# Three-piece float32 products on one Trainium2 core: the order of the products that share a weight tile

## The chip, the cores and the metric

The kernel runs on one NeuronCore of a Trainium2 chip. The metric is the device time of one launch in microseconds. The core's engines appear under their profile names: PE (TensorE, matrix products; PEld is its load of the stationary operand), DVE (VectorE), ACT (ScalarE), POOL (GpSimd) and SP (SyncE, which here only issues transfers).

## The reference

One layer of a bidirectional encoder over 256 tokens, all in float32, with model width 2048. Cut to its large products:

```python
h  = rmsnorm(x, mix_norm_pre)               # (256, 2048)
u  = h @ w_in                               # z 1024 | xbc 1536 | dt 32, pooling 1024
y  = cat(ssd_both_directions(u), pooled(u)) # (256, 2048): state space heads and pooling
x  = x + rmsnorm(y @ w_out, ...)
h  = rmsnorm(x, ...)
g, v = split(h @ w_ffn_up)                  # 2 x 5632
f  = gelu(conv3(g)) * v                     # (256, 5632)
x  = x + rmsnorm(f @ w_down, ...)
gate = sigmoid(rmsnorm(x, ...) @ w_ple_gate) # (256, 2048), computed with a tanh
out = x + rmsnorm(gate * (p @ w_ple), ...)
```

The weights come from HBM; the result must agree with the float32 reference closely.

## The kernel before

**Three products for one.** PE multiplies in a rounded float32 format. To keep float32 accuracy, every operand is split into a high part (the value rounded to that format) and a low part (the remainder). `split()` (L142 to L155) does it for a weight tile: ACT copies the raw tile into the high tile (L153), DVE subtracts that from the raw tile and gets the low tile (L154). High and low tiles come from two rings of five buffers each, the raw tiles from a ring of three that transfers on SP's queue fill. A product x·w is then the sum of three in PSUM: xh·wh, xh·wl and xl·wh. The product xl·wl is left out. `mm()` (L89 and L90) issues each of them; the profile therefore shows nearly all matmuls at L90 and tells them apart by their tiles. Names end in h and l: `dn_0h` is the high part of a w_down tile.

**The stages in time.** dtu (0 to 53 us; dt and pooling inputs, a loop of its own), xbc (53 to 143 us, with the small products of the state space part, such as seg, placed between), z (143 to 198 us), w_out (198 to 287 us, tiles woa, wos), ple and the transposes woxt, the up projection ga/va (293 to 788 us, `feature_pairs`), w_down (788 to 1011 us, tiles dna, dns, dn0s, dn1s), ple and the transposes dnxt, w_gate (1017 to 1106 us, tiles gt, gts), and the last norm with the output.

**feature_major** (L339 to L353) makes xbc with features on the partitions: the weight is the stationary operand, and the moving one is 256 tokens wide. A k tile gives 4 feature blocks of three products, 12 matmuls.

**token_major** (L305 to L337) makes z, w_out, ple, w_down and w_gate with 128 tokens on the partitions, in two token tiles t: a piece of x is stationary, and 512 columns of the weight move. Per half of 1024 columns, a k tile is 2 token tiles × 3 products × 2 column blocks, 12 matmuls. The variable q numbers the products: 0 is xh·wh, 1 is xh·wl, 2 is xl·wh. The last unit of a half (and the one that follows the last fast unit) runs instead bank by bank, over all k tiles of its group.

**seven_products** (L255 to L281) is used for the fast units of w_out, w_down and w_gate: seven products of blocks instead of eight, for a pair of k tiles, each in three pieces, 21 matmuls. Weight tiles are a, b, d and c in the order of their splits; b, d and c each serve two of the seven. x comes as the blocks a11, a12, a22 (from the split hidden tile hs, two buffers, written by ACT at L928 and DVE at L929) and the sums s1 to s4 (tile hd). `combine` adds the results up after the last fast unit.

**What sets the order.** The program is written in one order, and a scheduler then orders the instructions of each engine by readiness and priority, so that PE's order in the trace isn't quite that of the loops. Every engine works its list in order.

**The tail.** After w_gate's second half, each bank gets a tanh (ACT, L1154), a product (DVE, L1155), a square with a sum (ACT, L1162, the last one L1160) and a product with the norm's weight (DVE, L1163). `finish(t)` takes the norm of a token tile from POOL (go0m, go0r, L378 to L381; rest_of at L1106 to L1108) and writes vg with four steps on DVE (L1126).

Of the kernel before, what the change touches and what calls it, by code (L numbers as in the profile page):

```python
# [17 lines left out]
P = 128  # L18
L = 256
D = 2048  # L20
NK = D // P
# [32 lines left out]
def build(nc, a, out):  # L54
    x = a["x"][0]
# [5 lines left out]
    with tile.TileContext(nc) as tc, \  # L61
# [9 lines left out]
        def ins(r):  # L71
            return getattr(r, "ins", r)
# [10 lines left out]
        def main(name):  # L83
            return [pm.tile([P, 512], F32, tag="main", name=f"{name}_{i}") for i in range(2)]
# [4 lines left out]
        def mm(o, lhsT, rhs, start, stop):  # L89
            last["pe"] = ins(nc.tensor.matmul(o, lhsT, rhs, start=start, stop=stop, skip_group_check=True))  # L90
# [15 lines left out]
        acc, acc2 = [main(f"dtu{t}") for t in range(2)], main("dtu2")  # L106
# [10 lines left out]
        def load(dst, src, ahead=False):  # L117

            with tc.issue_after(last["dma"]) if last and not ahead else nullcontext():
                return ins(nc.sync.dma_start(dst, src))  # L120
# [36 lines left out]
        def raw(name, src=None):  # L157
            r = wp.tile([P, 2048], F32, tag="raw", bufs=3, name=name)
            if src is not None:
                last["dma"] = load(r, src, True)  # L160
            return r
# [25 lines left out]
        def put(dst, src, scale):  # L187
# [3 lines left out]
                    ins(nc.vector.scalar_tensor_tensor(lo, src, scale, hi.bitcast(F32),  # L191
                                                       op0=ALU.mult, op1=ALU.subtract)))

        work = []

        chain = {}
# [22 lines left out]
        def columns(acc):  # L219

            c = 0
            for o in acc:
                yield o, c
                c += o.shape[-1]
# [30 lines left out]
        def seven_products(name, stage, w, k0, c0, a_, acc, alt, start, stop):  # L255

            if (stage, c0, k0) in sums_:
                r = raw(f"{name}r")  # L260
                last["dma"] = load(r[:, 512:], w[c0 // 1024, k0 // 2][:, 512:], True)
                t, held = sums_[stage, c0, k0]
                if not held:
                    t = page(f"{name}t")
                    last["dma"] = load(t, sums_[stage, c0, k0][0], True)
            else:
                r = t = raw(f"{name}r", w[c0 // 1024, k0 // 2])
            b11 = split(f"{name}a", r[:, 512:1024], 512)
            b2 = split(f"{name}b", r[:, 1024:], 1024)
            if r is t:  # L270
                add_blocks(r)
            t42 = split(f"{name}d", t[:, 1024:], 1024)
            t31 = split(f"{name}c", t[:, :1024], 1024)

            for x, (wh, wl), c, o, own in (
                    ("a11", b11, 0, alt[0], True), ("a12", b2, 0, acc[0][0], False), ("a22", t42, 0, acc[1][0], False),
                    ("s4", b2, 512, acc[0][1], False), ("s2", t42, 512, alt[3], True), ("s1", t31, 512, alt[1], True),
                    ("s3", t31, 0, alt[2], True)):
                xh, xl = a_[x]
                for q, (xx, ww) in enumerate(((xh, wh), (xh, wl), (xl, wh))):  # L280
                    mm(o, xx, ww[:, c:c + 512], own and start and q == 0, own and stop and q == 2)  # L281

        def combine(name, acc, alt, cut):

# [20 lines left out]
        def token_major(name, w, c0, ks, get, acc, tail=1, fast=(), alt=None, sums=None, at=()):  # L305


            group, nu = [], len(ks) // 2
            for u in range(nu):
                if u in at:  # L310
                    at[u]()
                k0 = ks[2 * u]
                if u in fast:
                    if u == fast[0]:
                        alt = alt + [misc(f"{name}s{i}") for i in (2, 3)]
                    seven_products(f"{name}{k0}", name[:2], w, k0, c0, sums(k0), acc, alt, u == fast[0], u == fast[-1])
                    continue
                r = None if f"{name}{k0}_0" in ready else raw(f"{name}r{k0}", w[c0 // 1024, k0 // 2])
                for j in range(2):
                    group.append((k0 + j, *split(f"{name}{k0}_{j}", r and r[:, j * 1024:(j + 1) * 1024], 1024)))  # L320
                if nu - tail <= u < nu - 1:
                    continue

                order = [(t, o, g, q) for t in range(2) for o in columns(acc[t]) for g in group for q in range(3)] \
                    if u == nu - 1 or u - 1 in fast[-1:] else \
                    [(t, o, g, q) for g in group for t in range(2) for q in range(3) for o in columns(acc[t])]
                for t, (o, c), (k, wh, wl), q in order:
                    xh, xl = (v[:, t * P:(t + 1) * P] for v in get(k))
                    xx, ww = ((xh, wh), (xh, wl), (xl, wh))[q]
                    c = (c + 512 * (k + 1)) % 1024  # L330
                    mm(o, xx, ww[:, c:c + o.shape[-1]], k == ks[0] and q == 0, k == ks[-1] and q == 2)
                if u - 1 in fast[-1:]:
                    combine(name, acc, alt, nu - tail == u + 1 and tail > 1)
                group = []
                aside()
            if nu in at:
                at[nu]()  # L337

        def feature_major(name, w, get, acc):  # L339

            for u in range(4):
                r = raw(f"{name}r{u}", w[u])
                for j in range(2):
                    wh, wl = split(f"{name}{u}_{j}", r[:, j * 1024:(j + 1) * 1024], 1024)
                    for kk in range(2):
                        k = 4 * u + 2 * j + kk
                        xh, xl = get(k)
                        for f in range(4):
                            s = slice(kk * 512 + f * P, kk * 512 + (f + 1) * P)
                            for q, (ww, xx) in enumerate(((wh, xh), (wh, xl), (wl, xh))):  # L350
                                mm(acc[f // 2][:, f % 2 * L:(f % 2 + 1) * L], ww[:, s], xx,
                                   k == 0 and q == 0 and f % 2 == 0, k == NK - 1 and q == 2)
                aside()  # L353

        def feature_pairs(n, part, get, acc):
# [98 lines left out]
        for u in range(0, NK, 2):  # L454
            r = [wp.tile([P, 2048], F32, tag="raw", bufs=3, name=f"dtur{u}") if u else r0, page(f"dtur{u + 1}")]
            for j in range(2):
                k = u + j
# [17 lines left out]
            for j in range(2):  # L475
                k = u + j
                with tc.issue_after(front[0]), tc.issue_after(front[1]):
                    wh, wl = split(f"dtu{k}", r[j][:, :1056], 1056, ((352, 704), (704,))[k] if k < 2 else ())
# [480 lines left out]
        parts, slab = [], {}  # L959
# [47 lines left out]
        with in_order():  # L1007
            for _ in range(5):
                next_part()
            for n in range(NPIECES):  # L1010
                s, v, i = blocks[n // 4]
                if n % 4 == 0:
                    acc = main(f"{'gv'[v]}a{s}{i}")
# [117 lines left out]
        for half in range(2):  # L1131

            alt = [] if half else main(f"gts{half}")
            acc = [main(f"gt{half}{t}") for t in range(2)]
            alt += main(f"gts{half}") if half else []
            ks, fast = gt_ks[half], gt_fast[half]
# [7 lines left out]
            for t in range(2):  # L1144
                for n, (o, c0) in enumerate(columns(acc[t])):
                    c1 = c0 + o.shape[-1]
                    c = slice(half * 1024 + c0, half * 1024 + c1)
# [9 lines left out]
                    q = tiny(f"gq{t}{half}{n}", 1)  # L1157
# [84 lines left out]
```

## Time and profile before

| What | Value |
|---|---|
| time, median of 3 runs | 1117.4 us (1116.87 to 1118.18) |
| span of the profiled execution | 1115.6 us |
| granted PE clock, mean | 0.998 |
| PE / PEld busy | 1104.8 / 951.8 us |
| DVE busy | 957.5 us |
| ACT busy | 721.7 us |
| POOL busy | 68.5 us |
| HBM read / written | 297.48 / 48.76 MB |

The page gives the span from the first to the last instruction of one execution, 1115.6 us; that execution's own time isn't listed beside it, and the median of the timed runs is 1.8 us above the span. Busy times are sums over instructions of one engine. A matmul's record is longer than the distance to the next one, because matmuls are pipelined; the distance between starts is what counts. Where the profile shows a wait, it names the engine, tile and line whose end released the waiting instruction.

### The profile page before, as it was taken

How to read it: one execution, taken by the hardware profiler on the slowest of the kernel's cores; microseconds unless marked ns; L12 is line 12 of the kernel's file. 1: busy time of each engine (PE TensorE's matmuls, PEld its weight loads, DVE VectorE, ACT ScalarE, POOL GpSimd, SP SyncE). 2: the span in 40 equal slices, each digit the busy share in tenths (PEclk: the TensorE clock that was granted, in tenths of full speed). 3: DMA queues.
4: the chain of work that ended last, by engine and by line, in shares of the span. 5: the costliest groups of instructions: out<-in, count | busy, mean ns of one | idle time of the engine just before them, and what ended most of it. 6: DMA issues, size and time to landing. Idle time of an engine off the chain costs nothing.

```text
span 1115.6 us, 16022 instructions
## 1 busy us (share of the span) xinstructions
PE 1104.8 (99%) x5948; PEld 951.8 (85%) x5948; DVE 957.5 (86%) x1334; ACT 721.7 (65%) x1048; POOL 68.5 (6%) x140
## 2 busy tenths in 40 slices
PE   9999999999999999999999999999999999999997
PEld 9999988888888888888888888888888888877876
DVE  6478997799868898888888888888899999989895
ACT  6847662555775564665655645657589778867673
POOL 0200000100100000000000000000000000001001
PEclk9999999999999999999999999999999999999999
DMA  9752447454599999999899999999999899996763
GB/s 362 314 194 109 164 156 284 151 189 158 199 362 401 387 378 376 359 375 369 346 377 382 354 380 366 353 391 391 361 379 382 329 343 400 418 376 229 264 237 105
DMA packets 54943, 347.29 MB, mean 311 GB/s; under 512 B 6096, under 2 KB 6992, under 8 KB 20176
## 3 DMA queue, kind: packets, MB, share of 16 engines
q1 hardware_dynamic: 44064, 289.53, 67.3%
q0 software_dynamic: 10368, 56.10, 13.4%
q8 instruction: 47, 0.77, 0.3%
q10 hardware_dynamic: 432, 0.62, 0.2%
q14 instruction: 32, 0.26, 0.1%
HBM read 297.48 MB, written 48.76 MB: 310 GB/s over the span
## 4 chain that ended last, share of the span: by engine, by line
PE 94%; DVE 2%; ACT 1%; DMA 1%; issue 1%; POOL 0%; POOLq 0%; ACTq 0%; DVEq 0%
PE ga L90 22%; PE va L90 22%; PE dna L90 12%; PE woa L90 7%; PE xbc L90 5%; PE gt L90 5%; PE z L90 4%; PE dns L90 4%; PE dtu L90 4%; PE dn0s L90 2%; PE dn1s L90 2%; DMA dtur<-w_dtu 1%; PE pw L90 1%; PE yd L90 1%; PE gts L90 1%
## 5 line engine op out<-in xcount | busy, mean ns | idle before, releaser
L90 PE MATMUL ga<-wox,ug_0h 128*128 128x512 f32 x352 | 125.5, 395 | 0.0
L90 PE MATMUL ga<-wox,ug_1h 128*128 128x512 f32 x352 | 125.1, 394 | 0.0
L90 PE MATMUL va<-wox,uv_1h 128*128 128x512 f32 x352 | 124.8, 393 | 0.0
L90 PE MATMUL va<-wox,uv_0h 128*128 128x512 f32 x352 | 124.8, 393 | 0.0
L90 PE MATMUL ga<-wox,ug_1l 128*128 128x256 f32 x352 | 99.1, 282 | 0.0
L90 PE MATMUL va<-wox,uv_1l 128*128 128x256 f32 x352 | 99.1, 281 | 0.0
L90 PE MATMUL va<-wox,uv_0l 128*128 128x256 f32 x352 | 99.1, 281 | 0.0
L90 PE MATMUL ga<-wox,ug_0l 128*128 128x256 f32 x352 | 99.0, 281 | 0.0
L253 DVE TENSOR_TENSOR dnb<-dnb 128x512 f32<-128x512 f32 x128 | 88.3, 690 | 3.1
L90 PEld LDWEIGHTS va<-wox,uv_1h 128*128 128x128 f32 x352 | 66.1, 188 | 15.0
L90 PEld LDWEIGHTS va<-wox,uv_0h 128*128 128x128 f32 x352 | 66.1, 188 | 15.0
L90 PEld LDWEIGHTS ga<-wox,ug_1h 128*128 128x128 f32 x352 | 66.1, 188 | 15.0
L90 PEld LDWEIGHTS ga<-wox,ug_0h 128*128 128x128 f32 x352 | 66.1, 188 | 14.8
L90 PEld LDWEIGHTS ga<-wox,ug_0l 128*128 128x128 f32 x352 | 66.2, 188 | 0.1
L90 PEld LDWEIGHTS ga<-wox,ug_1l 128*128 128x128 f32 x352 | 66.2, 188 | 0.0
L90 PEld LDWEIGHTS va<-wox,uv_1l 128*128 128x128 f32 x352 | 66.2, 188 | 0.0
L90 PEld LDWEIGHTS va<-wox,uv_0l 128*128 128x128 f32 x352 | 66.2, 188 | 0.0
L928 ACT CAST hs<-hid 128x512 fp32r<-128x512 f32 x44 | 27.3, 621 | 21.9 <-PE dna L90 21.6
L244 POOL DMA_DIRECT2D dns<-dnb x30 | 16.3, 542 | 309.4 <-DVE dnb L253 309.4
L929 DVE TENSOR_TENSOR hs<-hid,hs 128x512 fp32r<-128x512 f32 x44 | 30.1, 685 | 5.9 <-ACT hs L928 5.9
L792 ACT CAST he<-he 128x512 fp32r<-128x512 f32 x13 | 8.1, 621 | 36.6 <-DVE he L791 36.6
L90 PE MATMUL dna<-dn_1h,hs 128*128 128x512 f32 x96 | 30.9, 393 | 0.0
(2242 smaller groups left out, 3214.8 us busy)
## 6 DMA issues: line engine op xcount, KB each, us to landing
dnb<-w_down SPq DMA_DIRECT2D x32, 1024.0 KB, 9.9
dns<-dnb POOLq DMA_DIRECT2D x30, 1024.0 KB, 6.9
hd<-hsum POOLq DMA_DIRECT2D x24, 512.0 KB, 8.3
zr<-w_z SPq DMA_DIRECT2D x8, 1024.0 KB, 4.8
dtur<-w_dtu SPq DMA_DIRECT2D x14, 528.0 KB, 8.9
wo0r<-w_out_ SPq DMA_DIRECT2D x7, 1024.0 KB, 4.8
dn1r<-w_down SPq DMA_DIRECT2D x7, 1024.0 KB, 6.6
hsum<-he POOLq DMA_DIRECT2D x13, 512.0 KB, 7.9
```

The lines of the kernel that those rows point to most:

```text
L90: last["pe"] = ins(nc.tensor.matmul(o, lhsT, rhs, start=start, stop=stop, skip_group_check=True))
L244: nc.gpsimd.dma_start(t, pg[0])
L253: nc.vector.tensor_add(v[:, i], v[:, i], v[:, j])
L792: nc.scalar.copy(o[:, :512], s[:, :512])
L928: nc.scalar.copy(t[:, :512], hid_part(k))
L929: nc.vector.tensor_sub(t[:, 512:], hid_part(k), t[:, :512].bitcast(F32))
```

## The change

Within the instructions that share a weight tile, the products come in another order: xh·wh and xl·wh first for all of them, xh·wl last. `LOW_LAST = (0, 2), (1,)` holds the two groups of q. In token_major a k tile is now, for both token tiles, q = 0 and q = 2 (8 matmuls), then q = 1 (4 matmuls); in bank-by-bank order, each bank takes all k tiles' q = 0 and 2, then all q = 1. feature_major does the same over its 4 feature blocks. In seven_products the list is written out: a11 (0, 2, 1); a12 (0, 2); a22 (0, 2); a12 (1); s4 (0, 2, 1); a22 (1); s2 (0, 2, 1); s1 (0, 2); s3 (0, 2); s1 (1); s3 (1). The flag that ends a PSUM group moves from q = 2 to q = 1. Lines behind the first insertion move down by one to six. dtu, ga/va and everything else keep their order.

```diff
--- before.py
+++ after.py
@@ -191,6 +191,7 @@
                     ins(nc.vector.scalar_tensor_tensor(lo, src, scale, hi.bitcast(F32),
                                                        op0=ALU.mult, op1=ALU.subtract)))
 
+        LOW_LAST = (0, 2), (1,)
         work = []
 
         chain = {}
@@ -272,13 +273,16 @@
             t42 = split(f"{name}d", t[:, 1024:], 1024)
             t31 = split(f"{name}c", t[:, :1024], 1024)
 
-            for x, (wh, wl), c, o, own in (
-                    ("a11", b11, 0, alt[0], True), ("a12", b2, 0, acc[0][0], False), ("a22", t42, 0, acc[1][0], False),
-                    ("s4", b2, 512, acc[0][1], False), ("s2", t42, 512, alt[3], True), ("s1", t31, 512, alt[1], True),
-                    ("s3", t31, 0, alt[2], True)):
+            parts = {"a11": (b11, 0, alt[0], True), "a12": (b2, 0, acc[0][0], False), "a22": (t42, 0, acc[1][0], False),
+                     "s4": (b2, 512, acc[0][1], False), "s2": (t42, 512, alt[3], True), "s1": (t31, 512, alt[1], True),
+                     "s3": (t31, 0, alt[2], True)}
+            for x, qs in (("a11", (0, 2, 1)), ("a12", (0, 2)), ("a22", (0, 2)), ("a12", (1,)), ("s4", (0, 2, 1)),
+                          ("a22", (1,)), ("s2", (0, 2, 1)), ("s1", (0, 2)), ("s3", (0, 2)), ("s1", (1,)), ("s3", (1,))):
+                (wh, wl), c, o, own = parts[x]
                 xh, xl = a_[x]
-                for q, (xx, ww) in enumerate(((xh, wh), (xh, wl), (xl, wh))):
-                    mm(o, xx, ww[:, c:c + 512], own and start and q == 0, own and stop and q == 2)
+                for q in qs:
+                    xx, ww = ((xh, wh), (xh, wl), (xl, wh))[q]
+                    mm(o, xx, ww[:, c:c + 512], own and start and q == 0, own and stop and q == 1)
 
         def combine(name, acc, alt, cut):
 
@@ -321,14 +325,14 @@
                 if nu - tail <= u < nu - 1:
                     continue
 
-                order = [(t, o, g, q) for t in range(2) for o in columns(acc[t]) for g in group for q in range(3)] \
+                order = [(t, o, g, q) for t in range(2) for o in columns(acc[t]) for qs in LOW_LAST for g in group for q in qs] \
                     if u == nu - 1 or u - 1 in fast[-1:] else \
-                    [(t, o, g, q) for g in group for t in range(2) for q in range(3) for o in columns(acc[t])]
+                    [(t, o, g, q) for g in group for qs in LOW_LAST for t in range(2) for q in qs for o in columns(acc[t])]
                 for t, (o, c), (k, wh, wl), q in order:
                     xh, xl = (v[:, t * P:(t + 1) * P] for v in get(k))
                     xx, ww = ((xh, wh), (xh, wl), (xl, wh))[q]
                     c = (c + 512 * (k + 1)) % 1024
-                    mm(o, xx, ww[:, c:c + o.shape[-1]], k == ks[0] and q == 0, k == ks[-1] and q == 2)
+                    mm(o, xx, ww[:, c:c + o.shape[-1]], k == ks[0] and q == 0, k == ks[-1] and q == 1)
                 if u - 1 in fast[-1:]:
                     combine(name, acc, alt, nu - tail == u + 1 and tail > 1)
                 group = []
@@ -345,11 +349,13 @@
                     for kk in range(2):
                         k = 4 * u + 2 * j + kk
                         xh, xl = get(k)
-                        for f in range(4):
-                            s = slice(kk * 512 + f * P, kk * 512 + (f + 1) * P)
-                            for q, (ww, xx) in enumerate(((wh, xh), (wh, xl), (wl, xh))):
-                                mm(acc[f // 2][:, f % 2 * L:(f % 2 + 1) * L], ww[:, s], xx,
-                                   k == 0 and q == 0 and f % 2 == 0, k == NK - 1 and q == 2)
+                        for qs in LOW_LAST:
+                            for f in range(4):
+                                s = slice(kk * 512 + f * P, kk * 512 + (f + 1) * P)
+                                for q in qs:
+                                    ww, xx = ((wh, xh), (wl, xh), (wh, xl))[q]
+                                    mm(acc[f // 2][:, f % 2 * L:(f % 2 + 1) * L], ww[:, s], xx,
+                                       k == 0 and q == 0 and f % 2 == 0, k == NK - 1 and q == 1)
                 aside()
 
         def feature_pairs(n, part, get, acc):
```

## The prediction

> **What bounds the kernel now.** I read the page first (share of each engine, then the chain that ended last), then the waits of TensorE (PE), then the busy time by stretch, and last the rows around each wait of PE.
>
> ```profile
> span 1115.6 us, 16022 instructions
> PE 1104.8 (99%) x5948; PEld 951.8 (85%) x5948; DVE 957.5 (86%) x1334; ACT 721.7 (65%) x1048; POOL 68.5 (6%) x140
> PE 94%; DVE 2%; ACT 1%; DMA 1%; issue 1%; POOL 0%; POOLq 0%; ACTq 0%; DVEq 0%
> ```
>
> PE is busy for 1104.8 of 1115.6 us and carries 94% of the chain. A busy PE can still be a slow one, so its pitch matters. The chain gives unbroken pieces, which I divide by their counts (start, length, engine, tile):
>
> ```profile
> 12.66 40.31 PE dtu L90 x249
> 66.89 5.71 PE xbc L90 x48
> 142.65 22.18 PE z L90 x96
> 886.79 22.15 PE dna L90 x96
> ```
>
> A matmul 512 wide starts every 22.18/96 = 231 ns, one 256 wide every 5.71/48 = 119 ns. The change keeps every matmul with its size, so as long as the pitch holds, only PE's idle time can change: the gaps inside the stages it touches, and the head and tail at either end. These are all the waits of PE (us in total, times, longest):
>
> ```profile
> PE gof L90 <- ACT godg L1117: 1.9, 1, 1.9
> PE dtu L109 <- POOL ident masks.py:199: 1.4, 1, 1.4
> PE gt L90 <- DVE gt_0l L154: 0.8, 1, 0.8
> PE dtu L90 <- DVE dtu2l L154: 0.5, 1, 0.5
> PE gt L90 <- DVE gt18bl L154: 0.4, 1, 0.4
> PE dna L90 <- ACT dn_0h L153: 0.3, 1, 0.3
> PE seg L90 <- ACT E L599: 0.2, 1, 0.2
> ```
>
> The dtu loop at the head isn't touched, and gof is the last product of all. So the change has 0.8 + 0.4 + 0.3 + 0.2 = 1.7 us of visible waiting in its reach. Only two of these waits are for a low part, the thing that it asks for later. The gain is capped near this sum; the loss isn't.
>
> **The change part by part.** No engine gains or loses an instruction: the built kernels hold the same instructions on all five engines, and POOL's and SP's are in the same order, so no DMA is added or moved past another on its queue. What moves is PE's order and, because the scheduler follows PE, parts of DVE's and ACT's.
>
> *Pitch.* The new order changes which operand repeats between neighbours. The pieces above repeat differently: dtu (352 columns) uses each piece of x for three or six matmuls in a row, z for two or four, xbc changes the loaded piece at two of three. Yet they lie on one line: between 119 ns at 256 and 231 ns at 512, it gives 161 ns at 352, and dtu has 40.31/249 = 162 ns, small gaps included. So the order costs nothing that these rows show: 0. The z and dna pieces differ by 0.3 ns a matmul; over the some 2,400 touched ones that would be 0.7 us either way, which I keep for the range.
>
> One rule speaks against the change. In token_major the stationary piece of x now changes six times for each k tile of 12 matmuls instead of four; z has 192/12 = 16 such k tiles. The Trainium skill, TensorE: Matmul & The Clock Gate, "Step-by-step: what each phase is for", says that loads are separate instructions so that one load can serve many matmuls; by it the sum would gain 32 loads in z alone. The rows have no such saving to lose: PEld counts 5948 loads for 5948 matmuls, and they lie beside the matmuls. The sum stays without them.
>
> *Normal k tiles (z, w_out, w_down, w_gate, xbc).* As written, the weight's low part was needed at the third of a k tile's 12 matmuls and is now needed at the ninth: 6 × 231 ns = 1.4 us later in token_major, 6 × 119 ns = 0.7 us in feature_major, less where the scheduler had already moved it. The high tile is free sooner, the low one at most 0.5 us later. Where PE didn't wait, this is worth 0: z, the output projection, most of xbc.
>
> *xbc with seg.* The one wait here is for ACT's E copy, not for a split:
>
> ```profile
> 89.52 0.57 ACT L599 COPY E<-seg 128x512 f32<-128x512 f32 x1
> 90.15 0.50 PE L90 MATMUL seg<-seg_x,seg_w 128*128 128x512 f32 x1 [0.19 <-ACT E L599]
> ```
>
> The built order puts 8 xbc matmuls between the two seg products where 11 stood. PE arrives 3 × 119 ns = 0.36 us sooner at a copy that ACT ends no sooner (it runs back to back there). The wait grows by 0.36 us; bounds 0 and +0.4. I take **+0.36**.
>
> *Seven-product units.* With 21 matmuls (21 × 231 ns = 4.86 us) to a unit, the low parts are asked for as written one to three matmuls later (the scheduler shifts some by one or two). The last use of the hs tile by a22 moves from the 9th to the 12th matmul, 3 × 231 ns = 0.69 us later; ACT's next hs (L928) waits for it.
>
> ```profile
> 788.00:900.00 112.00, 112.00 (x487) 90.97 (x487) 105.46 (x128) 90.66 (x115) 7.02 (x13) 1.00 0.94 356
> 900.00:1000.00 100.00, 99.66 (x431) 80.31 (x430) 93.64 (x115) 78.47 (x97) 6.15 (x11) 1.00 0.99 393
> L928 ACT CAST hs<-hid 128x512 fp32r<-128x512 f32 x44 | 27.3, 621 | 21.9 <-PE dna L90 21.6
> L929 DVE TENSOR_TENSOR hs<-hid,hs 128x512 fp32r<-128x512 f32 x44 | 30.1, 685 | 5.9 <-ACT hs L928 5.9
> ```
>
> The windows give PE, PEld, DVE, ACT and POOL busy, then clock and DMA share. PE fills the down projection while DVE works 94% of it. ACT's wait on PE is long, but the tile is for a later unit, and what DVE loses to it is 5.9 us over 44. In most units the scheduler now puts hs behind the d and c splits instead of ahead of them, so the later release delays nothing: 0. In dn126 to dn132 and dn138 hs still stands ahead; there the splits behind it may come 0.69 us later, but are asked for up to 0.69 us later: 0, with the rival below as the upper bound.
>
> *dn_0h after unit dn132.* This k tile follows a fast unit:
>
> ```profile
> 982.59 0.39 PE L90 MATMUL dn1s<-dn132ch,hd 128*128 128x512 f32 x1
> 983.26 1.20 PE L90 MATMUL dna<-dn_0h,hs 128*128 128x512 f32 x4 [0.28 <-ACT dn_0h L153]
> 984.52 0.73 PE L90 MATMUL dna<-dn_0l,hs 128*128 128x512 f32 x2
> 983.24 1.23 DVE L154 TENSOR_TENSOR dn_0l<-dn1r,dn_0h 128x1024 fp32r<-128x1024 f32 x1 [0.25 <-ACT dn_0h L153]
> ```
>
> From start to start PE loses 0.67 − 0.23 = 0.44 us to the high part. Four matmuls from 983.26 would end near 984.19, but the low part is ready at 984.47: 0.33 us more, of which 0.1 is the restart that both orders have. The low one goes, for eight matmuls now stand ahead of it. The high one shrinks by a matmul, since hs is released one matmul earlier in this unit. Together **−0.55**; bounds −0.77 (all of it) and +0.2 (hi 0.2 later).
>
> *End of w_down, start of w_gate.* Here come ple products, then transposes of the new hb (dnxt), then w_gate:
>
> ```profile
> 1005.27 0.63 PE L90 MATMUL ple<-ple_0h,pth 128*128 128x512 f32 x2
> 1010.59 0.40 PE L90 MATMUL dna<-dn_1h,hs 128*128 128x512 f32 x1
> 1013.86 0.38 PE L391 MATMUL dnxt<-ident,hb 128*128 128x128 f32 x2
> 1021.86 0.72 PE L90 MATMUL gt<-gt_0l,dnxh 128*128 128x512 f32 x2 [0.79 <-DVE gt_0l L154]
> 1020.59 1.22 DVE L154 TENSOR_TENSOR gt_0l<-gt0r,gt_0h 128x1024 fp32r<-128x1024 f32 x1
> ```
>
> Before, 13 ple products stood between w_down's last matmul and the first transpose; now 19 do, 6 × 231 ns = 1.4 us more. w_down's last matmul comes sooner by 0.55 (above), by 0.46 (the two ple products at 1005.27 no longer run inside it) and by an estimated 0.3 (the short stops there for low parts), 1.3 us in all. So the transposes stay within 0.1 us of where they were, and with them DVE's row of hb, dnxl and gt_0l, which ends near 1021.9 instead of 1021.81. PE has two more matmuls behind it when it comes to gt_0l, 0.46 us of work: in all it is 0.4 us ahead after this wait. Of that 0.55 is counted already, so this stage gives **+0.15**, and the saving of w_down's end is spent in a longer wait for gt_0l. Bounds −0.9 (the wait of 0.79 and its restart gone) and +0.9 (transposes 0.8 later).
>
> *gt18.*
>
> ```profile
> 1069.33 0.40 PE L90 MATMUL gts<-gt18ah,dnxl 128*128 128x512 f32 x1
> 1070.17 0.50 PE L90 MATMUL gt<-gt18bl,dnxh 128*128 128x512 f32 x1 [0.45 <-DVE gt18bl L154]
> ```
>
> PE loses 0.84 − 0.23 = 0.61 us and 0.1 at the restart. gt18bl is now asked for after seven matmuls of the unit instead of five, 0.46 us later, so that 0.15 us is left: **−0.55**; bounds −0.7 and −0.3.
>
> *The tail.* The last group of w_gate runs bank by bank. With high parts first and the last raw tile just landing, the built order draws high products of later banks ahead of the low ones of the first. Counting from the end, the banks of token tile 0 finish 1.0 and 2.7 us later than before, the third 0.8 later, the last two at the same place. Their epilogue is a chain of its own, which today runs right up to the end:
>
> ```profile
> 1078.94 16.73 PE gt L90 x73
> 1095.70 0.70 ACT gth L1154
> 1097.15 0.73 ACT gth L1162 x2
> 1098.05 1.07 POOL go0m L378
> 1100.16 2.75 DVE vg L1126 x4
> 1102.90 0.61 DVE gth L1155
> 1106.14 0.55 POOL gth L1108
> 1107.74 0.42 ACT L1160 ACTIVATE gth<-gth 128x257 f32<-128x257 f32 x1 [0.55 <-DVE gth L1155]
> ```
>
> Read from above: banks done, tanh (L1154), square (L1162), POOL's norm, four vg of token tile 0 on DVE, then the last tile's steps. The final square at 1107.74 waits for DVE; POOL's value, which it needs too, is ready at 1106.69, 1.05 us ahead. The first bank is done at 1078.94 + 16.73 = 1095.67 and the second two matmuls later, near 1096.2. With that at 1098.9, its tanh runs at 1099.1, its product and square end near 1101.2, POOL's two last steps near 1102.3: the four vg start 2.1 us late and end at 1105.0. Behind them DVE has the product of the third bank (0.61), one half as wide, and two vg; ACT has two squares ahead of the last tanh, which starts at 1107.0. POOL's value comes at 1108.0, the final square at 1108.0: **+0.28**. Bounds 0 (POOL quicker; the cover is that 1.05 us) and +1.4 (POOL's step as slow as its 1.07 us row once more).
>
> *Sum.* 0.36 − 0.55 + 0.15 − 0.55 + 0.28 = −0.31 us. The span would go from 1115.6 to 1115.3. The median of 1117.4 lies 1.8 us above the profiled span; I take what lies around the span as unchanged. 1117.4 − 0.3 = **1117.1 us**.
>
> **The rivals.** *All waits go.* If the low parts are the whole story and nothing replaces them, the lower bounds add up: −0.77 − 0.9 − 0.7 and 0 elsewhere, and the pitch's −0.7: −3.1 us, 1114.3. For it speaks that two of the four waits are for low parts; against it, that the wait at seg is for a copy, that at dn_0h for a high part, and that the transposes hold gt_0l back. Chance 0.16 for a gain above 0.2%.
>
> *hs starves DVE (slower).* In the fast units of w_down DVE has 0.94 × 4.86 = 4.57 us of work for 4.86 us of PE: 0.29 us to spare. Where hs stands ahead of the splits in ACT's and DVE's queues and its release is 0.69 us later, DVE loses 0.4 us per unit net, and PE waits as soon as the splits' own lead is used up. In the six or so units that keep that order it is some 2.4 us, 1119.8; with restarts and a longer wait at dn_0h about 1120.2; if all 32 fast units behaved so, 13 us, 1130. It decides when DVE's idle time in front of L929 grows from 5.9 us to above 8. Against it: the splits are asked for later by the same 0.69 us, and the scheduler moved hs back in most units. Chance 0.20. Upper bounds falling together at the transposes and in the tail (+0.9 + 1.4 + 0.4) would also pass 0.2%: 0.10.
>
> *It does little.* At dn_0h the scheduler already had four high products ahead of the first low one, half of what the change asks. If it reorders so wherever it matters, the time stays at 1117.4: 0.12.
>
> **How the numbers follow.** Forecast 0.42, no effect 0.12, all waits go 0.16, slower 0.20 + 0.10. A measurement of this kernel tells about 0.2%, 2.2 us, from no change; the forecast and the third rival both lie within it: same 0.54, faster 0.16, slower 0.30. The range: the terms at their upper ends give 0.4 + 0.2 + 0.9 − 0.3 + 1.4 + 0.7 = +3.3 us, 1120.7, which also takes in the six-unit case; at their lower ends the first rival's −3.1, 1114.3. Outside lie the 32-unit case and mixtures, some 0.15.
>
> **What would show it.** In the profile after: the waits for gt18bl and for dn_0l gone or under 0.2 us; the wait for gt_0l still there, at 0.8 to 1.6; seg's wait near 0.5; the four vg at L1132 (the same line, six lower) starting about 2 us later against the last gts product; PE's pitch in z at 231 ns. I am wrong if the pieces of z or dna change their pitch, if DVE's idle time before hs passes 8 us, or if a wait appears in a stage where I put 0.

## The result and the profile after

| What | before | after |
|---|---|---|
| time, median of 14 runs each | 1117.41 us (1116.84 to 1118.52) | 1119.36 us (1118.60 to 1120.46) |
| span of the profiled execution | 1115.6 us | 1117.9 us |
| time of the profiled execution | not listed | 1119.7 us |
| mean span of timed runs | 1115.25 us (108 runs, timed beside the experiments below) | 1117.34 us (the same 14) |

The ratio after to before is 1.0018, with a 95% interval of 1.0011 to 1.0025. The changed kernel is 2 us slower; 1117.1 us, 0.3 us faster, was forecast. The time outside the span scatters by over a microsecond from run to run, so the table of experiments below gives mean spans beside the medians.

The page of the kernel after, its first lines (span, then busy time and count of each engine):

```profile
span 1117.9 us, 16121 instructions
PE 1105.9 (99%) x5948; PEld 951.8 (85%) x5948; DVE 958.0 (86%) x1334; ACT 716.3 (64%) x1048; POOL 68.5 (6%) x140
```

Every engine has the same number of working instructions as before; the 99 that the page counts more are semaphore instructions (DVE has 549 instead of 448, ACT 433 instead of 435). PE has the same 5948 matmuls, yet it is busy 1.1 us longer, and the span grew by 2.3. The busy time alone doesn't show slower matmuls, for the records of matmuls overlap (e9_select below, whose span is shorter than that of the kernel before, has 1105.6 us). The waits and the distances between starts tell more. All waits of PE in the kernel after (us in total, times, longest):

```profile
PE gof L90 <- ACT godg L1123: 2.8, 1, 2.8
PE dtu L109 <- POOL ident masks.py:199: 1.4, 1, 1.4
PE gt L90 <- DVE gt_0l L154: 0.6, 1, 0.6
PE dna L90 <- DVE hs L935: 0.5, 1, 0.5
PE dnxt L397 <- DVE dnxl L191: 0.3, 1, 0.3
PE seg L90 <- ACT E L605: 0.2, 1, 0.2
```

The waits for gt18bl and dn_0h are gone from the list, as forecast (from start to start PE still loses 0.1 and 0.2 us there). A wait for **hs**, the low part of x, is new in the middle of w_down, and the last one, gof, grew from 1.9 to 2.8 us.

PE runs its 5948 matmuls in nearly one order in both kernels, so the start of the matmul at the same position can be compared through the whole span (after minus before; where neighbours are swapped it is good to 0.1 us):

| Stretch (time in the kernel before) | at its end | step |
|---|---|---|
| dtu, to 53 us | −0.52 | −0.52: not reached by the change, see below |
| xbc with seg, to 104 | −0.70 | −0.18 |
| z and w_out, to 273 | −0.73 | −0.03 |
| end of w_out, start of the up projection, to 345 | −0.49 | +0.24 |
| the up projection, to 803 | −0.51 | −0.02 |
| fast units of w_down's first half, 803 to 883 | −0.23 | +0.28 |
| turn from first to second half, 883 to 907 | +0.91 | +1.14 |
| fast units of the second half, 907 to 982.6 | +1.13 | +0.22 |
| dn_0h after dn132 | +0.57 | −0.56 |
| end of w_down, ple, dnxt, gt_0l, to 1032 | +0.83 | +0.26 |
| w_gate to gt18, to 1067 | +0.91 | +0.08 |
| gt18 | +0.44 | −0.47 |
| to the last gts, 1107 | +0.52 | +0.08 |
| tail: to gof | +1.40 | +0.88 |
| last outputs, to the end of the span | +2.29 | +0.9 |

The first step comes mostly from a wait for dtu2l of 0.5 us that the profile of before had and the profile after hasn't, in the dtu loop that neither kernel changes; the other kernels' first stretch differs from before's by +0.04 to −0.85 us, and none of them changes that loop. The last is the final output's transfer, 3.3 us from issue to landing before and 4.2 after; in the other kernels this step lies between −0.4 and +0.2 us. Without these two the change costs 1.9 us, and the mean spans of the runs say 2.1.

**The turn.** PE in the kernel after, around 898 us (start, length, instruction, count, and in brackets the idle time before it and its releaser):

```profile
898.32 0.63 PE L90 MATMUL dna<-dn_0h,hs 128*128 128x512 f32 x2
899.42 1.20 PE L90 MATMUL dna<-dn_0h,hs 128*128 128x512 f32 x4 [0.47 <-DVE hs L935]
```

The same view of the kernel before:

```profile
898.14 0.62 PE L90 MATMUL dna<-dn_0l,hs 128*128 128x512 f32 x2
898.60 0.63 PE L90 MATMUL dna<-dn_0h,hs 128*128 128x512 f32 x2
899.07 0.62 PE L90 MATMUL dna<-dn_0l,hs 128*128 128x512 f32 x2
899.53 1.09 PE L90 MATMUL dna<-dn_0h,hs 128*128 128x512 f32 x4
```

From the two products xh·wh at 898.32 to the next row are 1.10 us for 2 matmuls of 0.23: 0.64 us lost. The four products that wait are xl·wh. Before, four xh·wl (the two rows of dn_0l) stood ahead of them, and they had no wait; now these come behind, so PE asks for xl 4 matmuls, 0.93 us, sooner. With the restart behind it this place costs 0.75 us. Most of the rest of the 1.14 is a stop at 892.5 us, where PE waits 0.2 us for ACT's half of the same kind of split (0.3 us with its restart). DVE of the kernel after in the same stretch:

```profile
896.84 0.75 DVE L845 SCALAR_TENSOR_TENSOR dnm<-dna,rf0r,gffn 128x512 f32<-128x512 f32 x1 [0.29 <-ACT dnj L844]
898.02 0.75 DVE L845 SCALAR_TENSOR_TENSOR dnm<-dna,rf1r,gffn 128x512 f32<-128x512 f32 x1 [0.43 <-ACT dnj L844]
898.69 0.68 DVE L935 TENSOR_TENSOR hs<-hid,hs 128x512 fp32r<-128x512 f32 x1
```

and DVE of the kernel before:

```profile
898.52 0.68 DVE L929 TENSOR_TENSOR hs<-hid,hs 128x512 fp32r<-128x512 f32 x1
```

DVE does not make hs sooner here: the step stands behind the products of the first half's banks with the norm's weight (dnm), and each of those waits for ACT's square of the same bank (dnj). In the kernel before, hs ended at 898.52 + 0.68 = 899.20 and was asked for at 899.53: 0.33 us of slack. The new order asked for 0.93.

### The profile page after: what moved, and what is told of

Read it like the earlier page. It is cut to its first block, busy times and chain, and to the rows that moved or that the text cites. A ratio compares the mean times of both kernels' runs of the same rounds, so it can differ in the third digit from the quotient of the medians.

```text
span 1117.9 us, 16121 instructions
## 1 busy us (share of the span) xinstructions
PE 1105.9 (99%) x5948; PEld 951.8 (85%) x5948; DVE 958.0 (86%) x1334; ACT 716.3 (64%) x1048; POOL 68.5 (6%) x140
## 4 chain that ended last, share of the span: by engine, by line
PE 95%; ACT 1%; DVE 1%; DMA 1%; issue 0%; POOL 0%; POOLq 0%; ACTq 0%
PE ga L90 22%; PE va L90 22%; PE dna L90 12%; PE woa L90 7%; PE gt L90 5%; PE xbc L90 5%; PE z L90 4%; PE dns L90 4%; PE dtu L90 4%; PE dn0s L90 2%; PE dn1s L90 2%; PE ple L90 1%; DMA dtur<-w_dtu 1%; PE pw L90 1%; PE gts L90 1%; PE yd L90 1%
## 5 line engine op out<-in xcount | busy, mean ns | idle before, releaser
L994 ACT ACTIVATE fc<-gr,vt 128x256 f32<-128x256 f32 x44 | 26.1, 593 | 4.1 <-DVE gr L987 4.1
```

The source lines that it names most:

```text
L994: nc.scalar.activation(c[:, f], v[:, f], AF.Identity, bias=vec(V_FCB + 4 * s + 2 * i + f), scale=vec(w + NF))
```

## The experiments

| Run | kernel | median us (before beside it) | ratio, 95% interval | mean span (before 1115.25) |
|---|---|---|---|---|
| e1_seven | new order in seven_products alone | 1118.34 (1117.09) | 1.0013 [1.0004, 1.0021] | 1116.46 |
| e2_token | in token_major alone | 1118.56 (1117.09) | 1.0012 [1.0003, 1.0021] | 1116.35 |
| e3_feature | in feature_major alone | 1116.96 (1117.09) | 0.9998 [0.9989, 1.0007] | 1115.19 |
| e5_dn1_first_old | after, old order at the turn | 1118.84 (1117.17) | 1.0016 [1.0007, 1.0025] | 1116.91 |
| e6_both_old | e5, and the last group of w_gate old | 1119.22 (1117.09) | 1.0018 [1.0009, 1.0026] | 1116.84 |
| e7_both_old_pin | e6, and gof's first pair held at the end | 1118.55 (1117.17) | 1.0013 [1.0004, 1.0021] | 1116.63 |
| e4_tail_old_pin | after, last group old, pair held | 1118.95 (1117.16) | 1.0016 [1.0007, 1.0025] | 1116.99 |
| e8_seven_q021 | before, seven_products in order 0, 2, 1 | 1118.29 (1117.17) | 1.0009 [1.0001, 1.0018] | 1116.27 |
| e10_seven_q102 | before, seven_products in order 1, 0, 2 | 1117.54 (1117.16) | 1.0005 [0.9997, 1.0014] | 1115.91 |
| e9_select | new order at gt18's half and at dn_0h alone | 1116.75 (1117.17) | 0.9995 [0.9986, 1.0004] | 1114.83 |
| e11_select2 | e9, and w_down's last group | 1116.60 (1117.16) | 0.9996 [0.9987, 1.0005] | 1114.89 |
| e12_select3 | e9, and another order in unit dn132 | 1116.10 (1117.15) | 0.9992 [0.9983, 1.0001] | 1114.36 |

### Which function carries the loss

The theory: token_major loses at the turn and in the tail, seven_products gains at gt18 and loses in pitch. The rival: the waits are an accident of the three edits together.

e1_seven keeps the old loops of token_major and feature_major:

```diff
-  order = [... for qs in LOW_LAST for g in group for q in qs] ...   # token_major, feature_major
+  order = [... for g in group for q in range(3)] ...                # as in the kernel before
```

> Only seven_products has the new order; token_major and feature_major keep the old one. Theory A (the time goes to a wait of PE for the low part of hs at the first k tile of w_down's second half, +0.75 to 1.0 us, to the late banks of token tile 0 in the last group of w_gate, +0.9 us, and to a slightly longer pitch in w_down's fast units, +0.7 us; three waits of before give 1.0 us back): the first two come from token_major, so this kernel has the pitch (+0.7), the shorter wait for gt18bl (-0.4) and little else: 1117.4 to 1118.2 us. Rival B (hs is released later by a22 and stands behind the d and c splits in the fast units, which costs the time): this kernel carries nearly all of the change, 1119 us or more.

e2_token keeps the old list of seven_products and feature_major:

```diff
-  for x, qs in (("a11", (0, 2, 1)), ("a12", (0, 2)), ...):
+  for x, (wh, wl), c, o, own in (...): for q in 0, 1, 2             # as in the kernel before
```

> Only token_major has the new order. Theory A: a wait of PE for DVE's hs of 0.4 us or more near 898 us and banks of token tile 0 that end late (the second by 1.9 us); no longer pitch in the fast units (230.5 ns as before, not 231.6): 1118.0 to 1119.0 us. Rival B: the same as before, 1117.4 us.

e3_feature has the new order only in feature_major:

```diff
-  for f in range(4): for q in 0, 1, 2
+  for qs in LOW_LAST: for f in range(4): for q in qs
```

> Only feature_major (xbc) has the new order. Theory A and rival B: no effect, 1117.4 us within 0.4. The prediction on record gave +0.36 us for this part (a longer wait of seg).

feature_major costs nothing (−0.06 us of mean span). seven_products alone adds 1.2 us, more than expected (1118.34 us against at most 1118.2), and token_major alone 1.1; together they would make 2.3, and the kernel after has 2.1. By the positions of the matmuls the turn costs 1.15 us in e2_token and nothing in e1_seven, so it comes from token_major alone. The waits of PE in e2_token that matter here:

```profile
PE gof L90 <- ACT godg L1118: 1.9, 1, 1.9
...
PE dna L90 <- DVE hs L930: 0.5, 1, 0.5
PE gt L90 <- DVE gt18bl L154: 0.4, 1, 0.4
PE dna L90 <- ACT dn_0h L153: 0.3, 1, 0.3
```

The wait for hs belongs to token_major, the gain at gt18 does not, and gof is at 1.9 here and in e1_seven: the longer tail, which was expected of e2_token, needs both functions. In e1_seven:

```profile
PE dna L90 <- DVE hs L933: 0.9, 1, 0.9
PE dna L90 <- ACT dn_0h L153: 0.5, 1, 0.5
```

seven_products alone removes the wait for gt18bl, but the scheduler then puts the hs of w_down's last group behind dn_1l in DVE's queue, and PE waits for that hs at 1008 us. That wait is the kernel's own, not a part of the 2.1 us; so the two functions' costs add up only by chance.

### The wait for hs at the turn, and the tail

The theory: with the old order in the first two k tiles of w_down's second half, the wait of hs goes, and some 1 us with it; with the old order in w_gate's last group, the tail's 0.9 goes too. The rival: other queues hold PE back, and the gain is spent in another wait.

e5_dn1_first_old:

```diff
+  part_order = LOW_LAST if not (name == "dn1" and u < 2) else ((0, 1, 2),)
-  order = [... for qs in LOW_LAST ...]
+  order = [... for qs in part_order ...]
```

> The changed kernel with the old order in the first two units of w_down's second half only, where the low part of hs (x) was asked for four matmuls earlier. Theory A (the wait for DVE's hs near 898 us is caused by asking for the low part of x sooner): that wait of 0.64 us from start to start is gone, the one of 0.2 us on ACT's hs just before stays: span 0.6 to 0.9 us below the changed kernel's 1117.3, time about 1118.6. Rival C (DVE's hs is late by itself, because it stands behind other DVE work, and PE waits in either order): same wait, 1119.4.

e6_both_old adds the last group of w_gate:

```diff
+  part_order = LOW_LAST if not (name == "gt1" and u == nu - 1 or name == "dn1" and u < 2) else ((0, 1, 2),)
```

> The changed kernel, but with the old order in two places: the first two units of w_down's second half and the last group of w_gate's second half. Theory A: the wait for DVE's hs near 898 us is gone and the final chain from the last matmul of gts to the last product of gof is again 2.2 us instead of 3.1: 1.5 to 1.9 us below the changed kernel, 1117.3 to 1118.0 us. Rival B: no change against the changed kernel, 1119.4 us.

PE of e5_dn1_first_old at the turn (the view shown above for the kernel after):

```profile
898.30 0.62 PE L90 MATMUL dna<-dn_0l,hs 128*128 128x512 f32 x2
898.76 0.63 PE L90 MATMUL dna<-dn_0h,hs 128*128 128x512 f32 x2
899.23 0.40 PE L90 MATMUL dna<-dn_0l,hs 128*128 128x512 f32 x1
899.46 0.68 PE L90 MATMUL dna<-dn_0h,hs 128*128 128x512 f32 x2
```

PE runs through, so the wait comes from the order of these k tiles. By the positions of its matmuls the turn now costs 0.48 us instead of 1.14; of that, 0.3 is the stop at 892.5 us, in the last group of the first half, which keeps the new order here. But the mean span falls by only 0.43 us against the kernel after, less than the 0.6 to 0.9 expected. Two of e5's waits:

```profile
PE gof L90 <- ACT godg L1124: 2.8, 1, 2.8
...
PE dna L90 <- ACT dn_0h L153: 0.5, 1, 0.5
```

PE comes to dn_0h (984 us) earlier and waits there 0.5 us, where the kernel after shows no wait. That place now gives back 0.14 us instead of 0.56: of the 0.66 us won at the turn, 0.42 were handed on.

e6 did not do better than e5, against what I expected. Its wait at gof stayed at 2.7 us. The chain of e6 shows why:

```profile
1085.22 0.86 PE gof L90 x2
1086.08 10.56 PE gt L90 x46
```

With the old order the scheduler drew the first two gof products (hb times the identity) from 1107 us into the last group. There they hold up the banks by 0.86 us; at their old place they run beside the last epilogue. To take that accident away, the pair was held behind the last gts.

e7_both_old_pin is e6 with

```diff
-  mm(last_ps, ident, h[1][:, :512], True, False)
+  with tc.issue_after(last["pe"]):
+      mm(last_ps, ident, h[1][:, :512], True, False)
```

> The changed kernel with the old order in the first two units of w_down's second half and in the last group of w_gate's second half, and with the two products of gof that start the last bank (hb by ident) held behind the last matmul of gts, where they stood before. In the run without that hold they moved in front of the tail, and the time stayed high. Theory A (late banks of token tile 0 make the tail longer by 0.9 us, and hs costs 0.7 to 1.1): the tail from the last gts matmul to the last square is 1.40 us as before, and the span is 1115.3 to 1115.9, the time 1117.3 to 1118.0; what is left over the kernel before is the pitch of the fast units, 0.7 us, less the waits saved. Rival C: 1118.6 or more.

e4_tail_old_pin has this and the old order in the last group of w_gate, and the new order at the turn:

```diff
+  part_order = LOW_LAST if not (name == "gt1" and u == nu - 1) else ((0, 1, 2),)
```

> The changed kernel with the old order in the last group of w_gate's second half alone, and gof's first two products held behind gts. The wait for hs near 898 us stays. Theory A: the tail from the last gts matmul to the final square is 1.40 us again instead of 2.3, 0.9 less; against that the group waits 0.6 us for gtl, as it did in the kernel with both places old: span 1117.0 to 1117.2, 0.1 to 0.4 below the changed kernel's 1117.3. If the tail did not hang on the order of that group, it stays at 2.3 and the span is 1117.7 or more.

The waits of e4_tail_old_pin:

```profile
PE gof L90 <- ACT godg L1124: 1.9, 1, 1.9
...
PE dna L90 <- DVE hs L936: 0.5, 1, 0.5
PE gt L90 <- DVE gtl L154: 0.4, 1, 0.4
```

The tail is back at its old 1.9 us. In its place PE waits 0.4 us for gtl at 1085 us, the low part of a tile of the last group that the old order asks for early; with the restart PE loses 0.7 us there from start to start. Of the 0.9 us, 0.35 remain in the mean span, about twice its standard error. With both stages old and the pair held (e7), 0.7 of the kernel's 2.1 us are back, and the forecast for e7 (a span of 1115.3 to 1115.9) missed: by the positions of its matmuls the last group of w_gate now costs 0.8 us, the turn and the pitch of w_down's fast units some 0.5 each, and gt18 gives 0.5 back.

### The pitch of the fast units

In w_down's fast units PE never waits, yet the kernel after lost 0.5 us there. All matmuls that run in two stretches of that stage can be counted (window, its length, busy time of PE and matmuls in it; then clock, DMA share and GB/s). The kernel before:

```profile
800.00:884.00 84.00, 84.00 (x366) 1.00 0.98 375
905.00:978.00 73.00, 73.00 (x319) 1.00 1.00 397
```

The kernel after:

```profile
800.00:884.00 84.00, 84.00 (x364) 1.00 0.96 371
905.00:978.00 73.00, 73.00 (x318) 1.00 0.99 392
```

At the same clock of 1.00, two matmuls fewer fit into the first stretch and one fewer into the second. The mean distance of neighbours in the first went from 230.5 to 231.6 ns (362 pairs each; one distance of 329 ns in the kernel before is left out, and the kernel after has none like it). In the second it went from 230.7 to 231.3. Two things differ within a product of three: the high weight piece wh now moves twice in a row (xh·wh, xl·wh), and the stationary piece changes in another rhythm. The theory: the repeated moving piece costs the nanosecond. The rival: the stationary piece, or the interleaving of the products.

e8_seven_q021 takes the kernel before and changes only the order within each product, without interleaving:

```diff
-  for q in 0, 1, 2          # every product of seven_products
+  for q in 0, 2, 1
```

> Only the order inside each of the seven products changes (xh wh, xl wh, xh wl); the products stay in the old sequence and are not interleaved, everything else is old. If the pitch of w_down's fast units (231.6 ns in the changed kernel, 230.5 before) comes from the order inside a product, it is 231.5 here and the time 0.7 us above before, 1117.9; if it comes from interleaving the products, so that the last reader of each tile is spread out, it is 230.5 and the time 1117.1 to 1117.4, with the wait for gt18bl near 0.4 as before.

e10_seven_q102 keeps the stationary piece for two of three, as before (xh, xh, xl), but moves wh twice in a row:

```diff
-  for q in 0, 1, 2
+  for q in 1, 0, 2
```

> Only the order inside each of the seven products changes: xh wl, xh wh, xl wh. As before the change, the stationary piece stays for two of the three (xh, xh, xl); as in the changed kernel, the same moving piece of the weight (wh) comes twice in a row. If the longer pitch in w_down's fast units comes from the stationary piece changing with every matmul, it is 230.5 ns here and the time that of before plus any waits for the low parts, which are now asked for first. If it comes from reading the same moving piece twice in a row, it is 231.5 ns, and 0.7 us more. The low parts asked for first may bring new waits of PE for DVE, which I read apart from the pitch.

The same count in e10_seven_q102:

```profile
800.00:884.00 84.00, 84.00 (x364) 1.00 0.96 373
905.00:978.00 73.00, 73.00 (x317) 1.00 0.99 395
```

and in e9_select, whose w_down has the old order in these units:

```profile
800.00:884.00 84.00, 84.00 (x366) 1.00 0.96 371
905.00:978.00 73.00, 73.00 (x319) 1.00 0.99 398
```

Over the matmuls of the fast units in both stretches the mean distance is 231.4 to 231.7 ns in e8, e10 and all kernels with the new order in these units, and 230.5 to 230.6 in e2, e3, e9 and the others that keep the old one there. e8 shows that the interleaving isn't needed for it, e10 that the changed rhythm of the stationary piece isn't. What all orders with the longer distance share is that the same weight columns move in two matmuls in a row. The distance inside such a pair is not longer throughout (230.9 ns in the kernel after, 231.8 in e8, 229.7 in e10); the one from the pair's second matmul to the next is (232.5, 232.4 and 233.4 ns). But in these orders a repeated high piece also means that the low piece no longer stands between two high ones, so that the repeat itself is the cause is likely, not shown, and neither is why it costs a nanosecond. And it is not the only way in which order acts: in token_major, where two column blocks alternate in either order and nothing repeats, the distance fell a little. Here is z in the kernel after, from the chain that ended last:

```profile
141.96 22.10 PE z L90 x96
```

22.10/96 = 230 ns, before 22.18/96 = 231. e8 and e10 also show what seven_products gives without interleaving: e8 loses the wait for gt18bl, e10 the one for dn_0h, and each has a longer mean span than before all the same (e10's median alone would not tell it from before).

### New order only where a wait is

If the costs sit in stages that had no wait to lose, the new order in the stages around two waits alone, gt18 and dn_0h, should be faster than both kernels. feature_major, too, is as before in the three kernels that follow.

e9_select:

```diff
+  if stage != "gt" or c0 == 0: old list of seven_products     # new only in w_gate's second half
+  part_order = LOW_LAST if name == "dn1" and 2 <= u < nu - 1 else ((0, 1, 2),)
```

> The new order only where the kernel before waited for a split: the seven products of w_gate's second half (gt18) and the k tiles of w_down's second half that are neither its first two units nor its last. Theory A: the waits for gt18bl (-0.5) and for dn_0h with dn_0l (-0.3 to -0.55) go and no new one comes: span 1114.3 to 1114.8, time 1116.2 to 1116.7, faster than both kernels. Rival C: new waits for hs at other places take it back, 1117.1 or more.

e11_select2 adds w_down's last group, for the wait that e9 showed there:

```diff
-  ... if name == "dn1" and 2 <= u < nu - 1 ...
+  ... if name == "dn1" and u >= 2 ...
```

> As the selective kernel (new order for the seven products of w_gate's second half and for the k tiles of w_down's second half from the third unit on), but now with the last group of w_down too, where that kernel had a wait of 0.69 us for dn_0l. Theory A: that wait goes; some of it comes back in the wait for gt_0l, which hangs on the transposes: span 1114.3 to 1114.8 (selective: 1114.8, before: 1115.25), time 1116.2 to 1116.7. Rival C: the wait moves to hs or to the transposes in full, 1116.75 or more.

e12_select3 starts from e9 and lets unit dn132 run xl·wh last and xh·wl first, so that hs comes free three matmuls sooner for ACT's split of dn_0h:

```diff
+  qs = (1, 0, 2) if name == "dn132" else (0, 1, 2)
```

> The selective kernel, and in unit dn132 alone the products in the order xh wl, xh wh, xl wh. By the built order the last use of the hs tile by a22 then stands at the 12th matmul of that unit instead of the 15th, so that ACT's next hs and behind it dn_0h come 0.69 us sooner. If the wait for dn_0h near 982.6 us (0.44 us from start to start, 0.1 at the restart) hangs on that release, it goes: span 1114.3 (selective: 1114.8), time 1116.2, below both kernels. If dn_0h waits for its transfer or its buffer, nothing changes: 1114.8 and 1116.75.

Two waits of e9_select, then one of e11_select2:

```profile
PE dna L90 <- DVE dn_0l L154: 0.5, 1, 0.5
PE gt L90 <- DVE gt_0l L154: 0.4, 1, 0.4
```

```profile
PE gt L90 <- DVE gt_0l L154: 1.5, 1, 1.5
```

e9 is 0.4 us of mean span faster than the kernel before, just short of what was expected, with a new wait of 0.5 us for dn_0l. e11 takes that one away, and the wait for gt_0l grows from 0.4 to 1.5: the whole gain was handed on. gt_0l stands in DVE's queue behind the steps for hb and dnxl and starts at 1020.35 us, against 1020.26 in e9, though PE comes to it a microsecond sooner. e12, by its page:

```profile
span 1114.3 us, 16028 instructions
```

Its waits for dn_0l and gt_0l are those of e9, to the tenth. The one for dn_0h, 0.3 us in e9, is gone, by the way that was expected: ACT's hs starts at 980.46 us instead of 981.17, and its copy to dn_0h at 980.98 instead of 981.70. The mean span is 0.5 us below e9's and 0.9 below that of the kernel before. By the median it is 0.08% faster than the kernel before, with an interval that reaches just past 1; by the spans, which scatter less, it is the fastest of all kernels here.

## Why the prediction was wrong, step by step

**Normal k tiles, "worth 0": the step that failed.** I followed one operand of the moved products, the weight's low part, which is asked for later. The products that come in its stead, xl·wh, ask for the low part of x up to four matmuls, 0.93 us, sooner. The profile of before had the row that would have shown it: hs ends at 899.20 and is wanted at 899.53. The turn costs 1.1 us, the largest term, and it isn't in the sum. With the old order in the first two k tiles (e5) 0.66 of it goes, which shows the mechanism for that part; the stop for ACT's half at 892.5 us, 0.3, comes with token_major's new order (e2_token has it, e1_seven hasn't), and that it has the same cause is argued. This is the sign "a wait appears in a stage where I put 0".

**Pitch, 0 with ±0.7.** The value was wrong, the bound held: +0.28 and +0.22 us in w_down's fast units, 230.5 to 231.6 ns. That +0.5 fits into ±0.7 is partly luck, for the range was drawn from another difference, that of z and dna. I had compared stages by which loaded piece repeats; e10 keeps that rhythm and has the longer distance all the same. My note on the Trainium skill (TensorE: Matmul & The Clock Gate, on loads serving many matmuls) spoke of the loaded piece. The trace agrees that there was no saving to lose: PEld has 951.8 us before and after, and z, with its six changes in place of four, did not get slower (230 against 231 ns).

**dn_0h, −0.55.** Measured −0.56, and both parts as worked out: the wait for the low part went, the one for the high part shrank by 0.22. **gt18, −0.55.** Measured −0.47; 0.1 us of the wait is left from start to start.

**seg, +0.36.** Wrong in sign: the wait is 0.2 us as before, and the stretch gained 0.18. ACT's copy ended earlier too, which I had ruled out.

**End of w_down, start of w_gate, +0.15.** Measured +0.26, but not by the way forecast: gt_0l's wait was to grow and fell to 0.6, and a 0.3 us wait for dnxl joined it.

**Seven-product units and hs, 0, with the rival that hs starves DVE.** The rival is refuted. What DVE's hs step waited for in the kernel after (us, times):

```profile
  ACT hs L934: 3.6, 3
```

Its idle time fell from 5.9 to 3.6 us; the rival needed more than 8. The slower outcome came by another way, mostly through one hs at the turn, not through all.

**Tail, +0.28, bounds 0 and +1.4.** The mechanism was right and the size off: +0.88. The four vg were to start about 2 us late; DVE of the kernel after:

```profile
1102.92 2.74 DVE L1132 SCALAR_TENSOR_TENSOR vg<-vg,go0r,hb 128x512 f32<-128x512 f32 x4 [1.15 <-POOL go0r L387]
...
1107.82 0.42 DVE L1161 SCALAR_TENSOR_TENSOR gth<-gth,pl 128x256 f32<-128x256 f32 x1 [0.28 <-ACT gth L1160]
1108.28 0.42 DVE L1169 TENSOR_TENSOR vg<-gth,gple 128x256 f32<-128x256 f32 x1
```

They start 2.8 us later than before's 1100.16, 2.2 later against the last gts. POOL of the kernel after:

```profile
1107.20 1.10 POOL L1112 TENSOR_SCALAR go1m<-gq,go1m 128x1 f32<-128x1 f32 x2 [3.39 <-ACT gth L1168]
1108.38 0.74 POOL L1114 TENSOR_TENSOR gth<-go1m,half_up 128x1 f32<-128x1 f32 x1
```

Its value is ready at 1108.38 + 0.74 = 1109.12, while DVE's product is done at 1108.24; before, POOL was 1.05 us ahead. I had POOL's steps at their short durations, 0.27 us for each go1m and 0.55 for gth; the two go1m took 0.47 and 0.53 us and gth 0.74. That is 0.65 us more by my estimate, if nothing else held them, and 0.6 is what the term lacked. The bound of +1.4 had allowed for such a slow step. In e2_token, where the vg start at 1102.08, POOL's last step is short again, and the tail is the old one:

```profile
1107.56 0.55 POOL L1109 TENSOR_TENSOR gth<-go1m,half_up 128x1 f32<-128x1 f32 x1
```

So the slack on this path held a delay of 1.4 us there, and not the one of 2.2 us.

**Sum.** The measured steps without the first and the last are +1.9 us, against −0.31: the turn (+1.1), the pitch (+0.5) and the tail (+0.6 more than forecast) make up the 2.2 us between them; the small terms cancel. "Does little" and "all waits go" are both refuted: two waits went and others came.

## What to carry to other kernels

Moving one product later moves another sooner, so list the deadline of every operand, x's low part as well as the weight's, against the time at which its queue can deliver it: the slack of 0.33 us stood in the profile. A wait removed between pipelined queues is worth only what the next gate lets through (e11: a wait of 0.5 us removed, 1.1 us more at gt_0l; e5: 0.42 of 0.66 us lost again at dn_0h). A reorder is best confined to the places that wait: two such places, and one unit in another order, gave 0.9 us of span, where the same change everywhere cost 2.1.

## What the runs showed of the hardware

In a stream of matmuls 512 wide, orders in which the same columns move twice in a row ran at 231.4 to 231.7 ns a matmul in eight kernels, and those without such repeats at 230.5 to 230.6 in six: 0.5% of a stage that is all PE. The extra time lies mainly behind the repeated pair. Another property that these orders share could be the cause.

POOL's one-column steps took 0.27 or 0.55 us, and in some places more: 0.74 for gth here, 1.07 for go0m in the chain of the kernel before. The longer ones here run while DVE has a step with two SBUF inputs under way: gth from 1108.38 beside DVE's 1108.28 to 1108.70, the second go1m beside 1107.82 to 1108.24. The Trainium skill, SBUF — State Buffer, "SBUF: two separate sides", says that such a DVE step and a POOL step that reads SBUF lock each other out for a whole instruction. These rows agree with it. One does not quite: in e2_token a go1m step that starts at 1106.36, 0.14 us before the end of such a DVE step, takes the short 0.27 us. No run here isolates it.
